# Stick-breaking attention: one scan over both sigmoids against differences of v, and the causal mask as a GpSimd product instead of a matmul

## The chip, the cores and the metric

The kernel runs on one core of a Trainium2 chip. The metric is the device time of one execution in microseconds (us), the median of the runs shown. Engines are named as in the profile: PE is TensorE (PEld its weight loads), DVE is VectorE, ACT is ScalarE, POOL is GpSimd, SP is SyncE, which here issues the DMAs.

## The reference

One layer of a streaming encoder: half a SwiGLU feed-forward, a mixer of two head groups, another half SwiGLU, and a closing norm, for 1024 prompt rows and 32 rows of a running stream. The change touches one head group, the stick-breaking attention: 8 heads of width 64, strictly causal, and for the running stream 128 cached keys ahead of its own 32.

```python
def sb_weights_apply(q, k, v, q_pos, k_pos):
    z = jnp.einsum('bqhd,bkhd->bhqk', q, k) * SB_SCALE
    causal = k_pos[None, :] < q_pos[:, None]
    log_fail = jnp.where(causal, jax.nn.log_sigmoid(-z), 0.0)
    after = lax.cumsum(log_fail, axis=3, reverse=True) - log_fail
    w = jnp.where(causal, jnp.exp(jax.nn.log_sigmoid(z) + after), 0.0)
    return jnp.einsum('bhqk,bkhd->bqhd', w, v)
```

So the weight of key k is sigmoid(z_k) times the product of sigmoid(-z_j) over the later visible keys j, and the output is the sum of the weights times the rows of v. v itself and the normed k are outputs too.

## The kernel before

Rows lie along the free axis: x is eight tiles of 128 features by 1056 rows (1024 of the prompt, 32 of the running stream). Matmuls with weights run in three products of split halves (`mm3`, lines 118 to 120) over three chunks of 352 rows.

The eight attention heads go in four pairs, p = 0 to 3. `sb_project` projects q, k and v of a pair, `sb_operands` splits q and k into high and low halves and loads the cache, and `sb_items` lists the work of a pair: for each of its two heads eight blocks of 128 queries, block i against the L = 128 (i + 1) keys up to its own. A block passes through three steps:

- `Block.scores` (lines 1588 to 1609): z = qk in one or two PSUM pieces of at most 512 columns (L1600, L1601); a third matmul per block adds a bfloat16 mask of -1e30 to the last 128 columns (L1603). ACT makes two sigmoids of each piece, f of -z (L1604) and w of z (L1605). DVE multiplies f up from the right in place (the scan, L1607), and then multiplies w by the product that starts one key later (L1608); a 1 behind the last column (the memset on POOL, L1595) is the empty product.
- `Block.turn`: PE transposes w, up to four 128-column pieces into one PSUM tile `tr` (L1619); ACT and DVE split it into a high and a low half `wt` (L109 and L113). There are two `tr` buffers, which the transposes of norms (L1124) and of v (L1142, L1149) share.
- `Block.values`: PE sums `wt` times the rows `vs` of v over two query blocks (L1632).

`Sample` does the same for the running stream with 160 keys (L1650 to L1664, mask matmul L1658). The scores of a block are listed three blocks ahead of its transposes. `run` mixes the list with filler for PE: the projections of the next pair, the gates of the other head group, and for the last pair the output projection (`out_group`). On that, a scheduler with its own cost model and the buffers of each pool sets the final order of every engine, so that an edit moves instructions that it doesn't name. Every engine then works its list strictly in that order.

Two things lie on POOL in this stage besides the memsets: the power -1/2 of the norms (L1046, nr from nv), for which it waits for DVE, and the copies that spread such a result over a tile (L1100).

v is projected in `put_v`: ACT copies the three chunks into `vf` (L1480), one DMA writes it out (L1482), and `rows_of` transposes it into `vs`. The cached v comes by one DMA per pair (L1567).

Of the kernel before, what the change touches and what calls it, by code (L numbers as in the profile page):

```python
# [7 lines left out]

F32 = mybir.dt.float32
F32R = mybir.dt.float32r  # L10
BF16 = mybir.dt.bfloat16
AF = mybir.ActivationFunctionType
ALU = mybir.AluOpType
PSUM = bass.MemoryType.PSUM

P = 128
# [13 lines left out]
def cs(c):  # L30
    return slice(c * CW, (c + 1) * CW)
# [1431 lines left out]
def sb_project(S, A, p, norms=()):  # L1463


    nc = S.nc
    T = Ctx()
    q = T.q = S.x[p]
    T.k = T.v = None

    def put_k(c, ps):
        if c == 0:
            T.k = S.stage.tile([P, NR], F32, name="kf", tag="kf")
            T.nk = Norm(S, T.k, S.ones64, 2, S.vec[:, 1:2])
        nc.scalar.activation(T.k[:, cs(c)], ps, AF.Copy)

    def put_v(c, ps):
        if c == 0:
            T.v = S.stage.tile([P, NR], F32, name="vf", tag="vf")
        nc.scalar.activation(T.v[:, cs(c)], ps, AF.Copy)  # L1480
        if c == NCH - 1:
            nc.sync.dma_start(A["v"][p], T.v)  # L1482

    def put_q(c, ps):
        if c == 0:
            T.sq = square_buf(S)
        nc.scalar.activation(T.sq[:, cs(c)], ps, AF.Square)
        nc.vector.tensor_scalar(q[:, cs(c)], ps, S.vec[:, 0:1], 0.125, op0=ALU.mult, op1=ALU.mult)

    def scales(r):  # L1490

        T.rq = r
# [89 lines left out]
class Block:  # L1582
# [5 lines left out]
    def scores(self):  # L1588
        S, T, h, i = self.S, self.T, self.h, self.i
        nc = S.nc  # L1590
        L = (i + 1) * P
        qs = slice(i * P, L)
        f = S.big.tile([P, NR], F32, name="f", tag="f")
        w = S.big.tile([P, SEQ], F32, name="w", tag="b")
        nc.gpsimd.memset(f[:, L : L + 1], 1.0)  # L1595
        n = L if L <= 512 else L // 2
        for s0 in range(0, L, n):
            z = S.pz.tile([P, 512], F32, name="z", tag="z")
            last = s0 + n == L
            nc.tensor.matmul(z[:, :n], T.qh[h][:, qs], T.ks[h][:, s0 : s0 + n], start=True, stop=False)  # L1600
            nc.tensor.matmul(z[:, :n], T.ql[h][:, qs], T.ks[h][:, s0 : s0 + n], start=False, stop=not last)  # L1601
            if last:
                nc.tensor.matmul(z[:, n - P : n], S.identb, S.maskb, start=False, stop=True)  # L1603
            nc.scalar.activation(f[:, s0 : s0 + n], z[:, :n], AF.Sigmoid, scale=T.rn[:, i, h : h + 1])  # L1604
            nc.scalar.activation(w[:, s0 : s0 + n], z[:, :n], AF.Sigmoid, scale=T.rq[:, i, h : h + 1])  # L1605
        fr = f[:, 0:L][:, ::-1]
        nc.vector.tensor_tensor_scan(fr, fr, fr, 1.0, op0=ALU.mult, op1=ALU.bypass)  # L1607
        nc.vector.tensor_mul(w[:, :L], w[:, :L], f[:, 1 : L + 1])  # L1608
# [27 lines left out]
class Sample:  # L1636
# [7 lines left out]
    def scores(self):  # L1644
        S, T, W = self.S, self.T, self.W
        nc = S.nc
        z = S.pz.tile([P, 512], F32, name="zs", tag="z")
        f = S.tmp.tile([DEC, 2, W + 1], F32, name="fs", tag="fs", bufs=1)
        w = self.w = S.tmp.tile([DEC, 2, W], F32, name="ws", tag="ws", bufs=1)
        nc.gpsimd.memset(f[:, :, W : W + 1], 1.0)  # L1650
        zv = z[:DEC, : 2 * W].rearrange("p (h s) -> p h s", h=2)
        for h in range(2):
            qh, ql, kn = T.qh[h][:, SEQ:NR], T.ql[h][:, SEQ:NR], T.ks[h][:, SEQ:NR]
            nc.tensor.matmul(zv[:, h, :PAST], qh, T.kc[:, h], start=True, stop=False)
            nc.tensor.matmul(zv[:, h, :PAST], ql, T.kc[:, h], start=False, stop=True)
# [80 lines left out]
def body(tc, A):  # L1736
# [10 lines left out]
    with ExitStack() as top:  # L1747
# [70 lines left out]
        with ExitStack() as es:  # L1818
# [37 lines left out]
            def chores(slots):  # L1856
                slots.later(20, lambda: nc.vector.tensor_copy(S.identb, consts[:, 0]))
                slots.later(20, lambda: nc.vector.tensor_copy(S.maskb, consts[:, 2]))
                splits.plan(slots)

            gate_up(S, H, op, steps, None, None, lambda p, xd: downs[0].head(p, xd), A["x"], chores, (R, done))
# [234 lines left out]
def constants():  # L2096
    i = np.arange(P)
    ident = np.eye(P, dtype=np.float32)
    ones64 = np.where(i[:, None] // 64 == i[None, :] // 64, 1.0 / 64, 0.0)
    causal = np.where(i[None, :] >= i[:, None], -1e30, 0.0)  # L2100
    consts = np.stack([ident, ones64, causal], 1).astype(np.float32)
    reset = np.ones((P, NR), np.float32)
    reset[:, ::P] = 0.0
    s, t = i[:, None], i[None, :]
    masks = [(s >> (lv + 1) == t >> (lv + 1)) & ((s >> lv) % 2 == 0) & ((t >> lv) % 2 == 1) for lv in range(5)]
    even = masks[1] & (s % 2 == 0)
    masks = np.stack([masks[0], even, masks[1] & ~even] + masks[2:] + [s == t], 1).astype(np.uint32)
    return consts, reset, masks


def layouts(i):
# [36 lines left out]
    a["cv"] = c(i["cache_sb_v"].reshape(PAST, 4, P).transpose(1, 0, 2))  # L2148
# [42 lines left out]
```

## Time and profile before

| | us |
|---|---|
| median of three runs | 2094.55 (2091.72 to 2094.66) |
| span of the profiled execution, first to last instruction | 2092.9 |
| the stage with the four head pairs, from about 960 to 1320 in the profile | 360 |
| PE busy in this stage | 344.85 |
| DVE, ACT and POOL busy in this stage | 267.27, 204.98, 55.17 |

The profiled execution is given by its span; its own device time isn't listed beside it, and the median lies 1.65 us above that span. In the profile a group of instructions has its line, engine, operation, out<-in by the program's names, shape and count, then busy us and mean ns of one, then the idle time of the engine just before them and what ended it. A row of the timeline has start, duration, engine, line and the idle time before it. PE's matmuls overlap, so the busy time of a matmul is longer than what it keeps the next one waiting; the step from start to start shows that.

### The profile page before, as it was taken

The page shows a single profiled execution, that of the slowest core. Times are in us where ns is not written, and L with a number is a line of the kernel's source. Part 1 is how long each engine was busy: PE and PEld are TensorE (multiplying, and loading weights), DVE is VectorE, ACT ScalarE, POOL GpSimd, SP SyncE. Part 2 cuts the span into 40 slices and gives each one's busy share as a digit, 9 for nine tenths or more (in the row PEclk, how much of TensorE's full clock was granted, in tenths as well). Part 3 has the DMA queues.
Part 4 walks back from the last instruction along what each step waited for, and adds up shares of the span by engine and source line. Part 5 has one row for each costly group of instructions (what it writes and reads, how often), then busy time and mean ns, then how long its engine had stood idle before and what let it go on. Part 6 is the DMA issues. An engine that isn't in the chain of part 4 may idle for free.

```text
span 2092.9 us, 39194 instructions
## 1 busy us (share of the span) xinstructions
PE 2044.0 (98%) x15746; PEld 1982.8 (95%) x15746; DVE 1432.4 (68%) x2232; ACT 881.1 (42%) x1628; POOL 663.2 (32%) x586
## 2 busy tenths in 40 slices
PE   7999999999999999999999999999999999999998
PEld 6999999999999988888999988999999999999998
DVE  6877777765776756377667588696776666566655
ACT  5444444442233442336555466454443433322233
POOL 0144434336773200121122101001343343367720
PEclk9999999999999999999999999999999999999999
DMA  6367667769853111213314162332673434398622
GB/s 233 101 233 260 245 249 258 258 234 399 326 198 117 53 61 61 75 35 88 113 51 119 51 186 90 101 103 76 226 257 142 155 134 153 130 399 315 230 111 74
DMA packets 140580, 350.65 MB, mean 168 GB/s; under 512 B 12904, under 2 KB 34824, under 8 KB 136816
## 3 DMA queue, kind: packets, MB, share of 16 engines
q1 hardware_dynamic: 139824, 347.61, 46.7%
q8 instruction: 124, 2.03, 0.4%
q10 hardware_dynamic: 576, 0.54, 0.1%
q14 instruction: 56, 0.46, 0.1%
HBM read 216.70 MB, written 124.65 MB: 163 GB/s over the span
## 4 chain that ended last, share of the span: by engine, by line
PE 88%; DVE 7%; ACT 2%; DMA 2%; issue 1%; SPq 0%; DVEq 0%; ACTq 0%
PE acc_c L473 11%; PE acc_d L473 11%; PE acc_a L473 11%; PE acc_b L473 5%; PE pd_d L822 4%; PE pd_a L822 4%; PE pd_c L822 4%; PE pj L118 4%; PE acc L381 4%; PE pj L120 4%; PE pj L119 4%; PE pd L118 2%; PE pd L119 2%; PE pd L120 2%; PE pd_b L822 2%; DVE f L1607 2%
## 5 line engine op out<-in xcount | busy, mean ns | idle before, releaser
L473 PE MATMUL acc_a<-h,whl 128*128 128x264 f32 x1920 | 247.4, 285 | 0.3 <-DVE whl L51 0.3
L473 PE MATMUL acc_d<-part,S 128*128 128x264 f32 x1920 | 247.6, 285 | 0.0
L473 PEld LDWEIGHTS acc_a<-h,whl 128*128 128x128 f32 x1920 | 239.6, 188 | 0.5 <-DVE whl L51 0.5
L473 PEld LDWEIGHTS acc_d<-part,S 128*128 128x128 f32 x1920 | 239.8, 188 | 0.1
L118 PE MATMUL pj<-h,whl 128*128 128x352 f32 x576 | 205.4, 357 | 0.0
L120 PE MATMUL pj<-h,whl 128*128 128x352 f32 x576 | 189.9, 330 | 0.0
L119 PE MATMUL pj<-h,whl 128*128 128x352 f32 x576 | 189.4, 329 | 0.0
L51 DVE TENSOR_TENSOR x<-x 128x528 fp32r<-128x528 f32 (+1 forms) x188 | 156.0, 845 | 19.1 <-ACT x L50 19.0
L50 ACT ACTIVATE x<-x 128x528 fp32r<-128x528 f32 (+1 forms) x188 | 117.3, 634 | 119.2 <-DVE x L546 37.2
L526 POOL TENSOR_TENSOR x<-tc,x 128x528 f32<-128x528 f32 x60 | 100.3, 1672 | 186.2 <-DVE tc L525 148.8
L473 PE MATMUL acc_c<-h,A 128*128 128x264 f32 x960 | 123.7, 285 | 0.6 <-DVE u L492 0.6
L444 POOL TENSOR_TENSOR s<-wraw 128x512 f32<-128x512 f32 x38 | 60.8, 1599 | 200.3 <-DVE S L113 134.9
L473 PE MATMUL acc_c<-part,S 128*128 128x264 f32 x960 | 124.1, 285 | 0.0
L473 PE MATMUL acc_b<-h,S 128*128 128x264 f32 x960 | 123.6, 285 | 0.0
L473 PEld LDWEIGHTS acc_c<-h,A 128*128 128x128 f32 x960 | 119.7, 188 | 0.8 <-issue 0.8
L473 PEld LDWEIGHTS acc_c<-part,S 128*128 128x128 f32 x960 | 120.0, 188 | 0.0
L473 PEld LDWEIGHTS acc_b<-h,S 128*128 128x128 f32 x960 | 119.8, 188 | 0.0
L118 PEld LDWEIGHTS pj<-h,whl 128*128 128x128 f32 x576 | 110.1, 191 | 6.3 <-issue 2.5
L51 DVE TENSOR_TENSOR S<-s,S 128x512 fp32r<-128x512 f32 x152 | 114.1, 751 | 0.6 <-ACT S L50 0.6
L840 POOL TENSOR_TENSOR x<-x,u 128x528 f32<-128x528 f32 x64 | 98.3, 1553 | 45.3 <-DVE x L811 45.3
L119 PEld LDWEIGHTS pj<-h,whl 128*128 128x128 f32 x576 | 110.5, 192 | 1.0 <-issue 0.3
L50 ACT ACTIVATE S<-s 128x512 fp32r<-128x512 f32 x152 | 93.6, 623 | 42.0 <-POOL s L447 17.9
(389 smaller groups left out, 4869.8 us busy)
## 6 DMA issues: line engine op xcount, KB each, us to landing
part_spill<-x SPq DMA_DIRECT2D x112, 528.0 KB, 3.7
h<-part_spill SPq DMA_DIRECT2D x64, 528.0 KB, 10.7
part<-part_spill SPq DMA_DIRECT2D x48, 528.0 KB, 10.7
win_split<-x SPq DMA_DIRECT2D x44, 512.0 KB, 3.6
whl<-win_split SPq DMA_DIRECT2D x22, 1024.0 KB, 4.9
wraw<-w1g SPq DMA_DIRECT2D x22, 512.0 KB, 5.1
wraw<-w1u SPq DMA_DIRECT2D x22, 512.0 KB, 6.2
x<-win SPq DMA_DIRECT2D x44, 256.0 KB, 2.9
```

The source lines that it names most:

```text
L50: self.later(k, lambda: nc.scalar.activation(hi, src, AF.Copy))
L51: self.later(k + 1, lambda: nc.vector.tensor_sub(lo, src, hi.bitcast(F32)))
L118: nc.tensor.matmul(out, w[:, 0, wsl], a[:, 0, asl], start=first, stop=False)
L119: nc.tensor.matmul(out, w[:, 0, wsl], a[:, 1, asl], start=False, stop=False)
L120: nc.tensor.matmul(out, w[:, 1, wsl], a[:, 0, asl], start=False, stop=last)
L381: nc.tensor.matmul(out, self.w[i](k, a), quarter(S, k, b, j), start=k == 0 and n == 0, stop=k == KT - 1 and n == 2)
L444: eng.tensor_add(self.s1, a21, a22)
L473: nc.tensor.matmul(t[:, s, :SW], w[:, a, ks], m(k, b, s), start=fresh and k == 0 and n == 0, stop=k == 3 and n == 2, skip_group_check=not ...
L526: nc.gpsimd.tensor_mul(two(hid), t, sg)
L822: nc.tensor.matmul(t[:, s, :SW], w[:, u, k * P : k * P + P], b[:, v, ss(s)], start=fresh and k == 0 and i == 0, stop=k == 1 and i == 2, sk ...
L840: nc.gpsimd.tensor_add(x[r][h], x[r][h], u)
L1607: nc.vector.tensor_tensor_scan(fr, fr, fr, 1.0, op0=ALU.mult, op1=ALU.bypass)
```

## The change

With f = 1 - s (s the other sigmoid), the recurrence G_k = f_k G_(k+1) + s_k from the right gives the sum of all weights from key k on. The weight is G_k - G_(k+1), so the output is the sum of G_k times (v_k - v_(k-1)). The scan therefore takes both sigmoids (multiply by f, add w) and writes G into w; the transposes and the matmuls with v use G, and the rows of v are replaced by differences of neighbouring rows.

- In each block POOL multiplies the last 128 columns of w by a 0/1 mask (L1614 of the new file), the mask matmul goes, and so do the multiplication L1608 and the memset L1595. f needs no mask, since a masked w leaves the state of the scan at 0. The sample does likewise, with two products of 32 columns and no L1664.
- v goes through a new tile `vt`, one column wider than the chunk, that carries the last column of the chunk before. POOL copies that column, and takes the differences into `vf` (one 352-wide or 320-wide subtraction per chunk, and two short ones where the running stream begins, which use the last cached row, `cvl`). `v_out` is now written in three DMAs per pair out of `vt`.
- The cached v comes twice, once shifted by a row, in two DMAs, and POOL subtracts the one from the other.
- f has two buffers instead of three. The bfloat16 copies of the identity and the mask go (two DVE casts early in the program).

```diff
     def put_v(c, ps):
...
-        nc.scalar.activation(T.v[:, cs(c)], ps, AF.Copy)
-        if c == NCH - 1:
-            nc.sync.dma_start(A["v"][p], T.v)
+        t = S.tmp.tile([P, 1 + CW], F32, name="vt", tag="vt")
+        if c == 0:
+            nc.gpsimd.memset(t[:, 0:1], 0.0)
+        else:
+            nc.gpsimd.tensor_copy(t[:, 0:1], T.part[:, CW:])
+        nc.scalar.activation(t[:, 1:], ps, AF.Copy)
+        nc.sync.dma_start(A["v"][p][:, cs(c)], t[:, 1:])
+        n = CW if c < NCH - 1 else SEQ - c * CW
+        nc.gpsimd.tensor_sub(T.v[:, c * CW : c * CW + n], t[:, 1 : n + 1], t[:, :n])
+        if n < CW:
+            nc.gpsimd.tensor_sub(T.v[:, SEQ : SEQ + 1], t[:, n + 1 : n + 2], S.cvl[:, p : p + 1])
+            nc.gpsimd.tensor_sub(T.v[:, SEQ + 1 :], t[:, n + 2 :], t[:, n + 1 : CW])
+        T.part = t
...
-    cv = S.tmp.tile([P, P], F32, name="cv", tag="cv", bufs=1)
-    nc.sync.dma_start(cv, A["cv"][p])
-    put(T.vc, cv.unsqueeze(1))
+    cv = S.tmp.tile([P, 2, P], F32, name="cv", tag="cv", bufs=1)
+    for i in range(2):
+        nc.sync.dma_start(cv[:, i], A["cv"][p][i : i + PAST])
+    nc.gpsimd.tensor_sub(cv[:, 1], cv[:, 1], cv[:, 0])
+    put(T.vc, cv[:, 1:])
...
-        f = S.big.tile([P, NR], F32, name="f", tag="f")
+        f = S.big.tile([P, NR], F32, name="f", tag="f", bufs=2)
         w = S.big.tile([P, SEQ], F32, name="w", tag="b")
-        nc.gpsimd.memset(f[:, L : L + 1], 1.0)
...
-            nc.tensor.matmul(z[:, :n], T.ql[h][:, qs], T.ks[h][:, s0 : s0 + n], start=False, stop=not last)
-            if last:
-                nc.tensor.matmul(z[:, n - P : n], S.identb, S.maskb, start=False, stop=True)
+            nc.tensor.matmul(z[:, :n], T.ql[h][:, qs], T.ks[h][:, s0 : s0 + n], start=False, stop=True)
             nc.scalar.activation(f[:, s0 : s0 + n], z[:, :n], AF.Sigmoid, scale=T.rn[:, i, h : h + 1])
             nc.scalar.activation(w[:, s0 : s0 + n], z[:, :n], AF.Sigmoid, scale=T.rq[:, i, h : h + 1])
-        fr = f[:, 0:L][:, ::-1]
-        nc.vector.tensor_tensor_scan(fr, fr, fr, 1.0, op0=ALU.mult, op1=ALU.bypass)
-        nc.vector.tensor_mul(w[:, :L], w[:, :L], f[:, 1 : L + 1])
+        nc.gpsimd.tensor_mul(w[:, qs], w[:, qs], S.mask)
+        wr = w[:, :L][:, ::-1]
+        nc.vector.tensor_tensor_scan(wr, f[:, :L][:, ::-1], wr, 0.0, op0=ALU.mult, op1=ALU.add)
```

The scheduler's order changes from the first block of pair 0 to the end of the attention; ahead of that and behind it PE's order is the same. Lines of the changed file are up to 12 away from those before: L112 there is L113 here, L1045 is L1046, L1099 is L1100.

The list of DVE at the third to fifth block of pair 1 (keys 384, 512, 640) before; `f` and `w` are the sigmoids, `wt` the split of the transposed weights:

```order
L1607 SCALAR_TENSOR_TENSOR f<-f 128x384
L1608 TENSOR_TENSOR w<-w,f 128x384
L113 TENSOR_TENSOR wt<-tr,wt 128x128
L1607 SCALAR_TENSOR_TENSOR f<-f 128x512
L1608 TENSOR_TENSOR w<-w,f 128x512
L113 TENSOR_TENSOR wt<-tr,wt 128x2x128
L1607 SCALAR_TENSOR_TENSOR f<-f 128x640
L113 TENSOR_TENSOR wt<-tr,wt 128x3x128
```

And in the changed kernel, at the same place:

```order
L1616 SCALAR_TENSOR_TENSOR w<-f,w 128x384
L112 TENSOR_TENSOR wt<-tr,wt 128x128
L1616 SCALAR_TENSOR_TENSOR w<-f,w 128x512
L112 TENSOR_TENSOR wt<-tr,wt 128x2x128
L1616 SCALAR_TENSOR_TENSOR w<-f,w 128x640
L112 TENSOR_TENSOR wt<-tr,wt 128x3x128
```

The multiplication is gone, and each split of an earlier block (128 columns belong to the first block, 2x128 to the second) stands directly behind a scan.

POOL's list around the same place before, from the end of pair 0: seven memsets are those of the last two blocks of pair 0 and the first five of pair 1, and L1046 with its two copies is a norm of the filler:

```order
L1042 MEMSET nv 128x18
L1595 MEMSET f 128x1 x7
L1046 TENSOR_TENSOR nr<-nv,mhalf 128x18
L1100 COPY x<-nr 128x1024
L1100 COPY nL<-nr 32x128
L1042 MEMSET nv 128x9
```

In the changed kernel; L1614 is the mask product, and the first three of them belong to the last block of pair 0 and the first two of pair 1:

```order
L1488 TENSOR_TENSOR vf<-vt 128x320
L1490 TENSOR_TENSOR vf<-vt,cvl 128x1
L1491 TENSOR_TENSOR vf<-vt 128x31
L1614 TENSOR_TENSOR w<-w,consts 128x128 x3
L1045 TENSOR_TENSOR nr<-nv,mhalf 128x18
L1099 COPY x<-nr 128x1024
L1099 COPY nL<-nr 32x128
L1614 TENSOR_TENSOR w<-w,consts 128x128
L1041 MEMSET nv 128x9
L1614 TENSOR_TENSOR w<-w,consts 128x128 x3
```

The mask product of the third block of pair 1 (384 keys) stands behind the norm's power and both copies, where before only memsets stood.

More of the change, by code (lines that the diff above doesn't have):

```diff
@@ L10 @@
 F32R = mybir.dt.float32r
-BF16 = mybir.dt.bfloat16
 AF = mybir.ActivationFunctionType
@@ L1130, in square_buf @@
 def square_buf(S):
-    return S.nbuf[0] if S.nbuf else S.big.tile([P, NR], F32, name="sqb", tag="f")
+    return S.nbuf[0] if S.nbuf else S.big.tile([P, NR], F32, name="sqb", tag="f", bufs=2)
 def rows_of(S, src, put):
@@ L1598, in scores @@
             z = S.pz.tile([P, 512], F32, name="z", tag="z")
-            last = s0 + n == L
             nc.tensor.matmul(z[:, :n], T.qh[h][:, qs], T.ks[h][:, s0 : s0 + n], start=True, stop=False)
-            nc.tensor.matmul(z[:, :n], T.ql[h][:, qs], T.ks[h][:, s0 : s0 + n], start=False, stop=not last)
-            if last:
-                nc.tensor.matmul(z[:, n - P : n], S.identb, S.maskb, start=False, stop=True)
+            nc.tensor.matmul(z[:, :n], T.ql[h][:, qs], T.ks[h][:, s0 : s0 + n], start=False, stop=True)
             nc.scalar.activation(f[:, s0 : s0 + n], z[:, :n], AF.Sigmoid, scale=T.rn[:, i, h : h + 1])
             nc.scalar.activation(w[:, s0 : s0 + n], z[:, :n], AF.Sigmoid, scale=T.rq[:, i, h : h + 1])
-        fr = f[:, 0:L][:, ::-1]
-        nc.vector.tensor_tensor_scan(fr, fr, fr, 1.0, op0=ALU.mult, op1=ALU.bypass)
-        nc.vector.tensor_mul(w[:, :L], w[:, :L], f[:, 1 : L + 1])
+        nc.gpsimd.tensor_mul(w[:, qs], w[:, qs], S.mask)
+        wr = w[:, :L][:, ::-1]
+        nc.vector.tensor_tensor_scan(wr, f[:, :L][:, ::-1], wr, 0.0, op0=ALU.mult, op1=ALU.add)
         self.w = w
@@ L1647, in scores @@
         z = S.pz.tile([P, 512], F32, name="zs", tag="z")
-        f = S.tmp.tile([DEC, 2, W + 1], F32, name="fs", tag="fs", bufs=1)
+        f = S.tmp.tile([DEC, 2, W], F32, name="fs", tag="fs", bufs=1)
         w = self.w = S.tmp.tile([DEC, 2, W], F32, name="ws", tag="ws", bufs=1)
-        nc.gpsimd.memset(f[:, :, W : W + 1], 1.0)
         zv = z[:DEC, : 2 * W].rearrange("p (h s) -> p h s", h=2)
@@ L1656, in scores @@
             nc.tensor.matmul(zv[:, h, PAST:], qh, kn, start=True, stop=False)
-            nc.tensor.matmul(zv[:, h, PAST:], ql, kn, start=False, stop=False)
-            nc.tensor.matmul(zv[:, h, PAST:], S.identb[:DEC, :DEC], S.maskb[:DEC, :DEC], start=False, stop=True)
+            nc.tensor.matmul(zv[:, h, PAST:], ql, kn, start=False, stop=True)
         for h in range(2):
-            nc.scalar.activation(f[:, h, :W], zv[:, h], AF.Sigmoid, scale=T.rn[:DEC, NB, h : h + 1])
+            nc.scalar.activation(f[:, h], zv[:, h], AF.Sigmoid, scale=T.rn[:DEC, NB, h : h + 1])
             nc.scalar.activation(w[:, h], zv[:, h], AF.Sigmoid, scale=T.rq[:DEC, NB, h : h + 1])
-            fr = f[:, h, 0:W][:, ::-1]
-            nc.vector.tensor_tensor_scan(fr, fr, fr, 1.0, op0=ALU.mult, op1=ALU.bypass)
-        nc.vector.tensor_mul(w, w, f[:, :, 1 : W + 1])
+            nc.gpsimd.tensor_mul(w[:, h, PAST:], w[:, h, PAST:], S.mask[:DEC, :DEC])
+            wr = w[:, h][:, ::-1]
+            nc.vector.tensor_tensor_scan(wr, f[:, h][:, ::-1], wr, 0.0, op0=ALU.mult, op1=ALU.add)
     def turn(self):
@@ L1757, in body @@
         consts = const.tile([P, 3, P], F32, name="consts")
-        S.ident, S.ones64 = consts[:, 0], consts[:, 1]
-        S.identb = const.tile([P, P], BF16, name="identb")
-        S.maskb = const.tile([P, P], BF16, name="maskb")
+        S.ident, S.ones64, S.mask = (consts[:, n] for n in range(3))
         S.ones128 = const.tile([P, P], F32, name="ones128")
@@ L1763, in body @@
         S.vec = const.tile([P, 4], F32, name="vec")
+        S.cvl = const.tile([P, 4], F32, name="cvl")
         S.mhalf = const.tile([P, 2 * NB + 2], F32, name="mhalf")
@@ L1843, in body @@
             nc.sync.dma_start(S.vec, A["vec"])
+            nc.sync.dma_start(S.cvl, A["cvl"])
             downs = []
@@ L1854, in body @@
             splits = Splits(S, halves_of(jobs), (S.x[2], S.x[3]))
[L1856 to L1861, printed above, removed]
+            gate_up(S, H, op, steps, None, None, lambda p, xd: downs[0].head(p, xd), A["x"], splits.plan, (R, done))
             down = downs[0]
@@ L2099, in constants @@
     ones64 = np.where(i[:, None] // 64 == i[None, :] // 64, 1.0 / 64, 0.0)
-    causal = np.where(i[None, :] >= i[:, None], -1e30, 0.0)
+    causal = np.where(i[None, :] < i[:, None], 1.0, 0.0)
     consts = np.stack([ident, ones64, causal], 1).astype(np.float32)
@@ L2147, in layouts @@
     a["ck"] = c(i["cache_sb_k"].reshape(PAST, 4, P).transpose(1, 2, 0))
-    a["cv"] = c(i["cache_sb_v"].reshape(PAST, 4, P).transpose(1, 0, 2))
+    a["cv"] = c(np.pad(i["cache_sb_v"].reshape(PAST, 4, P).transpose(1, 0, 2), ((0, 0), (1, 0), (0, 0))))
+    a["cvl"] = c(i["cache_sb_v"].reshape(PAST, 4, P)[-1].T)
     a["state"] = i["state_gla"].reshape(2, P, P)
```

## The prediction, made before the changed kernel was run

> **What bounds the kernel now.** I read the page first, then the busy times of the stage with the attention, then the groups of instructions and the waits of that stage, and last the timeline at single places.
>
> ```profile
> span 2092.9 us, 39194 instructions
> PE 2044.0 (98%) x15746; PEld 1982.8 (95%) x15746; DVE 1432.4 (68%) x2232; ACT 881.1 (42%) x1628; POOL 663.2 (32%) x586
> ```
>
> PE is busy for 98% of the span. The change acts between about 960 and 1320 us, where the four head pairs lie; columns are the stretch, its length, and busy us of PE, PEld, DVE, ACT and POOL.
>
> ```profile
> 960.00:1320.00 360.00, 344.85 (x2343) 319.44 (x2342) 267.27 (x432) 204.98 (x445) 55.17 (x99) 0.99 0.31 94
> ```
>
> Here too PE is nearly full: 360 - 344.85 = 15.15 us are idle. So there are two ways to gain: issue less on PE, or take from the 15.15. Who makes PE wait:
>
> ```profile
> PE tr L1619 <- DVE wt L113: 5.4, 8, 1.6
> PE tr L1124 <- DVE wt L113: 4.1, 4, 1.7
> ...
> DVE f L1607 <- ACT f L1604: 22.3, 26, 2.0
> ```
>
> Nearly all of PE's own waits are for a `tr` buffer that DVE has not yet split into `wt`. DVE is late because scans and products stand in its list ahead of the split. DVE itself waited 22.3 us, 26 times, for ACT's first sigmoid: in these cases the scan stood at the head of its list and was not ready.
>
> **What goes from PE.** 64 mask matmuls in the blocks, 8 in the sample. A matmul's busy time overlaps its neighbours, so I take steps from start to start:
>
> ```profile
> 1024.77 0.40 PE L1601 MATMUL z<-ks,ql 128*128 128x512 f32 x1
> 1025.01 0.39 PE L1600 MATMUL z<-ks,qh 128*128 128x512 f32 x1
> ...
> 1025.23 0.40 PE L1601 MATMUL z<-ks,ql 128*128 128x512 f32 x1
> 1025.47 0.23 PE L1603 MATMUL z<-maskb,identb 128*128 128x128 bf16 x1
> 1025.51 0.41 PE L118 MATMUL pj<-h,whl 128*128 128x352 f32 x1
> 1025.75 0.32 PE L119 MATMUL pj<-h,whl 128*128 128x352 f32 x1
> ...
> 1026.07 0.32 PE L118 MATMUL pj<-h,whl 128*128 128x352 f32 x1
> 1026.23 0.32 PE L119 MATMUL pj<-h,whl 128*128 128x352 f32 x1
> ```
>
> Without a mask in between, L1601 keeps its follower 1025.01 - 1024.77 = 0.24 us, and L118 keeps L119 0.16 us: 0.40 together. With it, from L1601 to L119, it is 1025.75 - 1025.23 = 0.52. The mask matmul costs 0.12 us, though it is only 0.04 us until the next start: the rest is a slower first step behind it. 72 of them at 0.12 make 8.6 us. Bounds: 72 x 0.04 = 2.9 us below; above, the mean of a whole one (0.23, next row) x 64 = 14.7 us.
>
> ```profile
> L1603 PE MATMUL z<-maskb,identb 128*128 128x128 bf16 x64 | 14.7, 230 | 0.0
> L1607 DVE TENSOR_TENSOR_SCAN f<-f 128x128 f32<-128x128 f32 (+3 forms) x64 | 87.5, 1367 | 22.8 <-ACT f L1604 22.3
> L1608 DVE TENSOR_TENSOR w<-w,f 128x128 f32<-128x128 f32 (+3 forms) x64 | 49.4, 771 | 3.8 <-ACT f L1604 0.2
> L1605 ACT ACTIVATE w<-z,nr 128x384 f32<-128x384 f32 (+4 forms) x96 | 56.0, 584 | 0.0
> L1229 DVE TENSOR_TENSOR_SCAN B<-reset,B 128x1056 f32<-128x1056 f32 x2 | 4.7, 2358 | 0.1
> ...
> 1027.17 2.29 DVE L1607 TENSOR_TENSOR_SCAN f<-f 128x1024 f32<-128x1024 f32 x1 [0.24 <-ACT f L1604]
> 1029.49 0.69 DVE L113 TENSOR_TENSOR wt<-tr,wt 128x512 fp32r<-128x512 f32 x1
> ```
>
> **What goes from DVE, and what the scan then waits for.** The 64 products L1608 go, 49.4 us of DVE. The new scan has the form of L1229 (two inputs, multiply and add): 2358 ns for 1056 columns is 2.23 ns each, and 2.29 us for 1024 is the same, so the 87.5 us stay. But the scan must now wait for the second sigmoid as well (0.58 us, so far hidden beside the scan) and for the mask product on POOL. POOL's nearest rows:
>
> ```profile
> L786 POOL TENSOR_TENSOR s<-wraw 128x256 f32<-128x256 f32 x32 | 24.4, 764 | 22.4 <-DMA wraw<-w1d 12.5 <-DMA wraw<-w2d 10.0
> L111 POOL TENSOR_TENSOR h<-hf,h 128x352 fp32r<-128x352 f32 x12 | 13.4, 1124 | 66.6 <-ACT h L109 66.6
> L1046 POOL TENSOR_TENSOR nr<-nv,mhalf 128x18 f32<-128x18 f32 x11 | 37.8, 3433 | 54.2 <-DVE nv L1044 54.2
> ```
>
> 128 columns are half of L786's 256: an estimate between 0.38 (half of 764) and 0.76 us; I take 0.5. A free scan thus starts 0.58 + 0.5 = 1.1 us later than now and the block is done 1.1 - 0.77 = 0.3 us later on the mean, while DVE at the head of its list stands idle for what it used to compute. For the transposes that is harmless where they lie some us behind. It hurts where a split stands directly behind a long scan, as at 1029.49 above, where PE was already waiting. There are eight scans of 1024 columns; I put 2 us on PE for them (nothing if PE's slack holds, 8 x 1.1 = 9 us if all hit).
>
> Against that, DVE has 49.4 us less to do. It gains where DVE runs without a gap, as in the last block of all, where the next split comes behind the product:
>
> ```profile
> 1308.41 0.67 DVE L113 TENSOR_TENSOR wt<-tr,wt 128x512 fp32r<-128x512 f32 x1
> 1308.99 1.22 DVE L1608 TENSOR_TENSOR w<-w,f 128x1024 f32<-128x1024 f32 x1
> ```
>
> I take 5 of the 15.15 us back, what four such products last (4 x 1.22); bounds 0 and, with all of PE's waiting gone, 15.
>
> f has two buffers instead of three, so ACT's first sigmoid of a block waits for the scan two blocks earlier. Where blocks follow every 2 to 3 us that can hold ACT, and the copies listed behind; I put 1 us, between 0 and 3.
>
> **POOL's list.** So far it hardly mattered when POOL did anything in a block. Now 64 scans wait for it, and in its list some of the masks stand behind a norm's power and its two copies. The third block of pair 1 before:
>
> ```profile
> 1051.30 3.22 POOL L1046 TENSOR_TENSOR nr<-nv,mhalf 128x18 f32<-128x18 f32 x1 [2.10 <-DVE nv L1044]
> 1054.58 1.46 POOL L1100 COPY x<-nr 128x1024 f32<-128x1024 f32 x1
> 1055.98 0.75 POOL L1100 COPY nL<-nr 32x128 f32<-32x128 f32 x1
> ...
> 1052.09 0.57 ACT L1605 ACTIVATE w<-z,nr 128x384 f32<-128x384 f32 x1
> ...
> 1052.22 0.96 DVE L1607 TENSOR_TENSOR_SCAN f<-f 128x384 f32<-128x384 f32 x1 [0.38 <-ACT f L1604]
> 1053.31 0.56 DVE L1608 TENSOR_TENSOR w<-w,f 128x384 f32<-128x384 f32 x1
> ...
> 1051.10 0.34 PE L1601 MATMUL z<-ks,ql 128*128 128x384 f32 x1
> ...
> 1055.56 0.49 PE L1619 MATMUL tr<-consts,w 128*128 128x128 f32 x3
> ```
>
> w is ready at 1052.66, but the mask comes only behind the last copy, at about 1056.7, and ends at 1057.2; the scan of 384 columns takes 0.96 us, so the transposes that ran at 1055.56 can run at about 1058.2: PE waits 2.6 us. The split of the first block stands behind that scan too. Pair 2 has the same order; there I put 1.5 us, a choice between nothing and the same. The others of the eleven powers stand where a later block's mask is not yet due or its transposes lie several blocks off; 1 us together. POOL: 5 us, between 0 (masks slip in ahead, or PE's slack covers it) and 11 x 2.6 = 29 us.
>
> **The differences of v.** POOL gets 12 subtractions of about 1.1 us (L111's row) and small ones. ACT writes the last chunk, and the transposes of v follow:
>
> ```profile
> 951.87 0.46 ACT L1480 ACTIVATE vf<-pj 128x352 f32<-128x352 f32 x1
> 955.14 0.60 PE L1142 MATMUL tr<-consts,vf 128*128 128x128 f32 x4
> ...
> 1024.26 0.46 ACT L1480 ACTIVATE vf<-pj 128x352 f32<-128x352 f32 x1 [0.15 <-PE pj L120]
> 1043.77 0.60 PE L1142 MATMUL tr<-consts,vf 128*128 128x128 f32 x4
> ```
>
> From the ACT's end it is 2.8 us in pair 0 and 19 us in pair 1, so 1.1 to 1.5 us of POOL are covered; I cost them at nothing. Without that cover it would be 4 x 1.5 = 6 us. The three `v_out` DMAs and the second cache DMA are on SP, whose later entries are weights loaded far ahead; nothing. What does count is that a subtraction, or the wait for a chunk, can stand in POOL's list ahead of a mask; that is within the 5 us.
>
> Sum: -8.6 (PE) - 5 (DVE) + 2 (splits behind scans) + 1 (f) + 5 (POOL) = -5.6 us. The span goes from 2092.9 to 2087.3; the median lies 1.65 us above the span, so 2089.0 us in round numbers.
>
> **A rule that speaks against it.** Two products of one size next to each other:
>
> ```profile
> 970.57 0.69 DVE L1608 TENSOR_TENSOR w<-w,f 128x512 f32<-128x512 f32 x1
> ...
> 1055.34 1.25 DVE L1608 TENSOR_TENSOR w<-w,f 128x512 f32<-128x512 f32 x1
> ```
>
> The second ran while POOL copied (1055.98 above) and took 0.56 us longer. The Trainium skill, page "SBUF — State Buffer", section "Who interferes with whom", says that a VectorE instruction with two SBUF inputs and a GpSimd instruction that reads SBUF lock each other out for a whole instruction, the later one waiting. By that rule, to which these two rows agree, the memsets before were harmless and the new masks and subtractions are not.
>
> **Rivals.**
>
> *Scans and POOL take turns* (that rule at work). A mask that comes during another block's scan ends only behind it, and a subtraction holds a scan. Then each of the 64 masks adds its 0.5 us to DVE's chain: 32 of the 49.4 us are given back, DVE's relief of 5 us becomes about 2, and with the 12 subtractions delaying some scans PE gets 1 us more to wait. -5.6 + 4 = -1.6: 2093.0 us. For it: the row of 1.25. Against it: a scan that is next in line can't start before the one ahead ends anyway.
>
> *DVE was the brake.* Splits come sooner, PE's waits mostly go, and POOL's powers fall into slack: -8.6 - 8 = -16.6, about 2078.0 us. For it: PE's waits are for DVE. Against it: the scan now starts 1.1 us later and waits for two engines.
>
> *POOL becomes the brake, slower.* If every power in front of a mask stops DVE for its 3.4 us and more, and PE for 2 us on the mean over eleven of them, that is 22 us instead of 5: -5.6 + 17 = +11.4, about 2106.0 us. It decides from (8.6 + 5 - 3 + 4.2) / 11 = 1.3 us of PE per power. For it: from z (1051.10) to the transposes (1055.56) PE leaves the third block 4.5 us, and power and copies alone take 5.4. Against it: scores are listed three blocks ahead, and with 22.3 us of waiting already at the head of DVE's list PE itself waited 1.7 us at most.
>
> **How the numbers follow.** A measurement of this kernel tells 0.2% from no change, 4.2 us: faster is below 2090.4, slower above 2098.7. Chances: the forecast 0.45, of which two thirds end below 2090.4; DVE as the brake 0.15; taking turns 0.20, of which a tenth ends below 2090.4; POOL as the brake 0.20, of which a tenth stays within 0.2%. Faster: 0.30 + 0.15 + 0.02 = 0.47; slower: 0.18; same: 0.35. The bounds of the terms, which don't all meet, and most of the rivals give 2079 to 2100; beyond lie the ends of the first and last case, about 0.2 together.
>
> **What would show it.** Right: no L1603; PE's z steps shorter by 0.12 a block; scans at 2.23 ns a column; DVE busy in the stage lower by about 50 us, with more waiting for POOL's w; PE idle in the stage between 15 and 22 us, the new waits at the third blocks of pairs 1 and 2. Wrong: scans that take longer than 2.29 us for 1024 columns, PE's idle time below 10 or above 25 us, waits of PE for vf, or a time above 2098.7 us.

## The result, and the profile after

| | before | after |
|---|---|---|
| median, us | 2093.6 (2091.72 to 2094.66, 4 runs) | 2110.0 (2109.39 to 2111.77, 4 runs) |
| ratio to before | | 1.008 (95%: 1.0069 to 1.0092) |
| span of the profiled execution, us | 2092.9 | 2107.6 |

The change makes the kernel slower by 16.4 us. The prediction said 2089.0 us, with bounds of 2079 and 2100. All times here are medians of fast runs; one run further below, of before without the mask, was slow (2196.46 us at a clock of 0.849) and is not counted. The last PE instruction of the attention ends at 1317.96 us before and at 1333.40 after, 15.4 us later; in all the spans of the two profiled executions differ by 14.7. So the loss arises in the attention. The same stretch as in the prediction, after the change, in the same columns (stretch, length, busy us of PE, PEld, DVE, ACT, POOL, granted clock):

```profile
960.00:1320.00 360.00, 330.13 (x2174) 312.57 (x2173) 214.26 (x351) 198.11 (x433) 95.71 (x132) 0.96 0.30 91
```

PE is idle for 360 - 330.13 = 29.9 us where it was 15.15; the limit that the prediction set for "wrong" was 25. DVE is busy for 53 us less, as foreseen. POOL has 40 us more, and the granted clock is 0.96 in place of 0.99. Who waits for whom between 960 and 1340 us, with the total in us, the number of waits and the longest; PE's rows are put first:

```profile
PE tr L1627 <- DVE wt L112: 10.1, 7, 2.3
PE av L1640 <- DVE wt L112: 4.5, 3, 3.2
PE tr L1123 <- DVE wt L112: 4.4, 3, 1.9
PE tr L1677 <- DVE wt L112: 4.2, 1, 4.2
...
DVE w L1616 <- POOL w L1614: 67.8, 42, 4.8
DVE w L1616 <- POOL nv L1041: 4.4, 1, 4.4
POOL nr L1045 <- DVE nv L1043: 36.0, 10, 9.3
```

Read upwards from the scan's rows. The scan (L1616) waits 72 us for POOL, where the scan before waited 22.3 us for ACT. DVE works its list in order, so the split of other blocks' transposes (L112) stands behind the waiting scan, and PE waits for the split. Two groups of the same stretch tell why POOL is late:

```profile
L1616 DVE TENSOR_TENSOR_SCAN w<-f,w 128x128 f32<-128x128 f32 (+3 forms) x64 | 88.9, 1391 | 72.5 <-POOL w L1614 67.8 <-POOL nv L1041 4.4
L1614 POOL TENSOR_TENSOR w<-w,consts 128x128 f32<-128x128 f32 x64 | 31.4, 492 | 210.9 <-ACT w L1613 210.8
L1045 POOL TENSOR_TENSOR nr<-nv,mhalf 128x18 f32<-128x18 f32 (+1 forms) x11 | 35.5, 3227 | 36.1 <-DVE nv L1043 36.0
```

The mask itself takes 0.49 us, as estimated, and the scan is as long as it was (1391 ns on the mean, 1367 before). But eleven powers of 3.2 us on the mean (nine of 18 columns at 3.5 us, two of 9 columns at 1.8) stand in the same list as the masks. One of the places, the twelfth block of pair 1, where the transposes fell back by 5.5 us against before:

```profile
1105.31 3.22 POOL L1045 TENSOR_TENSOR nr<-nv,mhalf 128x18 f32<-128x18 f32 x1 [2.00 <-DVE nv L1043]
...
1106.24 0.68 ACT L1613 ACTIVATE w<-z,nr 128x512 f32<-128x512 f32 x1
...
1108.59 1.04 POOL L1099 COPY x<-nr 128x1024 f32<-128x1024 f32 x1
1108.68 0.28 PE L1640 MATMUL av<-wt,vs 128*128 128x256 f32 x1
...
1109.57 0.28 POOL L1099 COPY nL<-nr 32x128 f32<-32x128 f32 x1
...
1109.87 0.86 POOL L1614 TENSOR_TENSOR w<-w,consts 128x128 f32<-128x128 f32 x2
1110.35 1.46 DVE L1616 TENSOR_TENSOR_SCAN w<-f,w 128x512 f32<-128x512 f32 x1 [4.79 <-POOL w L1614]
1111.73 0.39 DVE L112 TENSOR_TENSOR wt<-tr,wt 128x256 fp32r<-128x256 f32 x1
...
1112.18 0.90 PE L1640 MATMUL av<-wt,vs 128*128 128x256 f32 x3 [3.22 <-DVE wt L112]
```

w is ready at 1106.92, the mask begins at 1109.87, behind the power and its two copies. DVE stands for 4.79 us at the scan, a split that PE needs stands behind it, and PE issues nothing from 1108.7 to 1112.2. Then a second price follows. Four single microseconds and the seven behind them, in the columns of the stretch above:

```profile
1109.00:1110.00 1.00, 0.00 (x0) 0.00 (x0) 0.00 (x0) 0.31 (x1) 1.00 (x4) 1.00 0.00 0
1110.00:1111.00 1.00, 0.00 (x0) 0.00 (x0) 0.65 (x1) 0.00 (x0) 0.73 (x2) 1.00 0.00 0
1111.00:1112.00 1.00, 0.00 (x0) 0.00 (x0) 1.00 (x2) 0.00 (x0) 0.00 (x0) 0.64 0.04 8
1112.00:1113.00 1.00, 0.82 (x4) 0.82 (x5) 1.00 (x2) 0.00 (x0) 0.00 (x0) 0.50 0.00 0
...
1112.00:1119.00 7.00, 6.82 (x28) 6.73 (x29) 3.20 (x5) 3.36 (x7) 0.46 (x1) 0.56 0.01 2
```

The third column from the right is PE's clock. The trace has it at half from 1111.3 to 1118.1 us, so PE comes back to half speed. It looks busy there, but does less: three of the 128x256 matmuls of `av` take 0.90 us at 1112.18, where thirteen took 1.65 at 1102.77, at full clock.

### The profile page after: what moved, and what is told of

Read it like the earlier page. It is cut to its first block, busy times and chain, and to the rows that moved or that the text cites. A ratio compares the mean times of both kernels' runs of the same rounds, so it can differ in the third digit from the quotient of the medians.

```text
span 2107.6 us, 38968 instructions
## 1 busy us (share of the span) xinstructions
PE 2041.6 (97%) x15674; PEld 1987.2 (94%) x15674; DVE 1385.6 (66%) x2162; ACT 881.3 (42%) x1628; POOL 708.7 (34%) x626
## 4 chain that ended last, share of the span: by engine, by line
PE 87%; DVE 5%; ACT 2%; issue 2%; DMA 2%; POOL 2%; SPq 0%; DVEq 0%; POOLq 0%; ACTq 0%
PE acc_a L472 11%; PE acc_c L472 11%; PE acc_d L472 11%; PE acc_b L472 5%; PE pd_d L821 4%; PE pd_a L821 4%; PE pd_c L821 4%; PE pj L117 4%; PE acc L380 4%; PE pj L118 4%; PE pj L119 4%; PE pd L117 2%; PE pd L119 2%; PE pd L118 2%; PE pd_b L821 2%
## 5 line engine op out<-in xcount | busy, mean ns | idle before, releaser
L50 DVE TENSOR_TENSOR x<-x 128x528 fp32r<-128x528 f32 (+1 forms) x188 | 156.1, 846 | 19.3 <-ACT x L49 19.2
L1616 DVE TENSOR_TENSOR_SCAN w<-f,w 128x128 f32<-128x128 f32 (+3 forms) x64 | 88.9, 1391 | 72.5 <-POOL w L1614 67.8
```

The source lines that it names most:

```text
L50: self.later(k + 1, lambda: nc.vector.tensor_sub(lo, src, hi.bitcast(F32)))
L1616: nc.vector.tensor_tensor_scan(wr, f[:, :L][:, ::-1], wr, 0.0, op0=ALU.mult, op1=ALU.add)
```

## The experiments

Theory 1: the mask product in POOL's list, behind long instructions, holds the scan; the scan at the head of DVE's list holds the splits; PE waits. Rivals: A, f has only two buffers; B, the v differences and their waits hold POOL; C, the scan has to wait for the second sigmoid in any case. Ratios are to before, on the same chip. The last two columns split the mean span into what the granted clock can have taken at most, span x (1 - mean clock), and the rest. The clock is on record to three digits, so the split of one run is good to 1 us. Edits are shown in part; the lines left out are named or marked by three dots.

| kernel | median us | ratio (95%) | clock's part, us | rest, us |
|---|---|---|---|---|
| before (four sets of 11 to 29 runs) | 2092.6 to 2094.6 | 1 | 9.1 to 10.2 | 2082.2 to 2082.7 |
| after | 2110.0 | 1.0080 (1.0069 to 1.0092) | 20.0 | 2088.5 |
| after, mask by matmul | 2090.6 | 0.9982 (0.9974 to 0.9991) | 10.3 | 2078.3 |
| after, mask on DVE | 2090.7 | 0.9983 (0.9975 to 0.9992) | 13.4 | 2075.7 |
| after, power left out | 2086.9 | 0.9965 (0.9952 to 0.9978) | 10.0 | 2075.4 |
| before, power left out | 2092.3 | 0.9989 (0.9981 to 0.9998) | 9.3 | 2081.2 |
| after, power in three | 2101.1 | 1.0032 (1.0019 to 1.0044) | 15.1 | 2083.4 |
| before, with POOL product | 2109.6 | 1.0080 (1.0064 to 1.0096) | 14.8 | 2093.9 |
| after, v differences on DVE | 2112.6 | 1.0090 (1.0077 to 1.0104) | 20.6 | 2090.3 |
| before, no mask | 2090.4 | 0.9985 (0.9976 to 0.9994) | 10.1 | 2078.3 |
| after, root on DVE | 2100.4 | 1.0028 (1.0019 to 1.0038) | 15.9 | 2082.9 |
| the same, w first | 2092.8 | 0.9990 (0.9981 to 1.0000) | 13.2 | 2077.5 |
| before, two f buffers | 2095.2 | 1.0001 (0.9991 to 1.0012) | 10.8 | 2082.2 |
| after, mask on DVE, w first | 2086.7 | 0.9959 (0.9946 to 0.9972) | 10.4 | 2074.3 |

**The mask back on PE.**

```diff
...
+                nc.tensor.matmul(z[:, n - P : n], S.identb, S.maskb, start=False, stop=True)
...
-        nc.gpsimd.tensor_mul(w[:, qs], w[:, qs], S.mask)
```

The sample and the constants go back likewise.

> After, but with the causal mask put back as a matmul of -1e30 on PE; POOL has no mask product, the scan, the two f buffers and the v differences stay. Theory 1 (the mask product in POOL's list holds the scan, the scan holds the splits, PE waits): the 67.8 us that scans wait for POOL go to zero, PE's idle time between 960 and 1320 us falls from 29.9 to under 20 us, the low-clock stretches become as few as before (6.8 us lost or less), and the time is 2084 to 2094 us although the matmuls cost some 8.6 us. Rival A (the two f buffers): ACT and the scans still wait, over 2100 us. Rival B (the v differences and their waits on POOL): the v transposes and PE still wait, over 2100 us. Rival C (a scan that must wait for the second sigmoid at all, at the head of DVE's list): scans wait for ACT w for over 50 us and the time stays above 2100 us.

Measured: 2090.6 us, 19 us less than after. No scan waits for POOL; PE's idle time is 12.2 us:

```profile
960.00:1320.00 360.00, 347.78 (x2382) 323.77 (x2381) 221.23 (x368) 206.81 (x448) 60.97 (x61) 0.99 0.30 93
```

The scans now wait for the second sigmoid:

```profile
DVE w L1619 <- ACT w L1617: 45.4, 44, 2.3
```

Two f buffers, the v differences and the wait for w are all still there, and the kernel is faster than before. So neither A nor B nor C makes the loss by itself.

**The mask on DVE.**

```diff
-        nc.gpsimd.tensor_mul(w[:, qs], w[:, qs], S.mask)
+        nc.vector.tensor_mul(w[:, qs], w[:, qs], S.mask)
```

The sample likewise.

> After, but with the mask product on DVE, in front of the scan, instead of on POOL. Theory 1: no scan waits for POOL, DVE gets 64 products of 128x128 (0.2 to 0.3 us each, 13 to 19 us of the 53 that it was relieved of), no mask matmul on PE; PE's idle time between 960 and 1320 us falls to 10 to 18 us and the time to 2076 to 2090 us. Rivals A to C (f's buffers, v differences, the wait for the second sigmoid): the product now waits for the second sigmoid at the head of DVE's list, nothing else is cured, and the time stays above 2100 us.

Measured: 2090.7 us, just above theory 1's range, with PE idle for 17.7 us. On DVE the product is shorter than on POOL, and the 19.2 us of the 64 take part of DVE's relief:

```profile
L1614 DVE TENSOR_TENSOR w<-w,consts 128x128 f32<-128x128 f32 x64 | 19.2, 300 | 35.2 <-ACT w L1613 34.8
```

**The power left out, in after and in before.** Order and number of all instructions stay.

```diff
-    nc.gpsimd.tensor_tensor(r.rearrange("p b g -> p (b g)"), v, S.mhalf[:, :n], op=ALU.pow)
+    nc.gpsimd.tensor_tensor(r.rearrange("p b g -> p (b g)"), v, S.mhalf[:, :n], op=ALU.mult)
```

> After, with the power of the norms on POOL replaced by a plain product of the same operands: the power is left out of the computation, the order on all engines is the same. If the 3.2 us of the powers are what holds the masks behind them, each of the eleven gives back some 3 us to the mask behind it and the loss of 16 us shrinks to under 6: 2094 to 2100 us, with most of the low-clock stretches gone. If what holds POOL is its own waiting in order (for DVE's nv, 36.0 us in 10 waits, and for ACT's vt, 16.9 us), the waits stay and the time falls by less than 5 us: 2105 to 2110.

> Control: before, with the same power left out. No block waits for POOL there, only a norm's apply and the sigmoid scales do: 2090 to 2094 us, within 0.2% of before. If it gains more than 4 us, the powers were in the path before the change too, and the gain of the same edit in after counts only by the difference.

Measured: after falls to 2086.9 us, 23 us less and lower than either theory gave; before only by 0.11%, 2.3 us. The place shown above, in this kernel:

```profile
1102.24 0.23 POOL L1045 TENSOR_TENSOR nr<-nv,mhalf 128x18 f32<-128x18 f32 x1 [2.00 <-DVE nv L1043]
1102.53 1.04 POOL L1099 COPY x<-nr 128x1024 f32<-128x1024 f32 x1
...
1103.17 0.68 ACT L1613 ACTIVATE w<-z,nr 128x512 f32<-128x512 f32 x1
...
1103.93 0.46 POOL L1614 TENSOR_TENSOR w<-w,consts 128x128 f32<-128x128 f32 x1
1104.43 1.23 DVE L1616 TENSOR_TENSOR_SCAN w<-f,w 128x512 f32<-128x512 f32 x1 [1.94 <-POOL w L1614]
```

POOL still waits for DVE's nv (42.1 us in the stretch) and the scans still wait 48.0 us for POOL, in waits of at most 2.6 us. So what cost was the power, and not the sum of the waits. Whether it was the length of one instruction or POOL's load, which falls with it by 31 us, this run can't tell; the power in three, below, can.

**One part alone, in before.** POOL multiplies and the mask matmul stays; besides, one early operation on DVE makes the 0/1 mask.

```diff
+        nc.gpsimd.tensor_mul(w[:, qs], w[:, qs], S.mask)
         fr = f[:, 0:L][:, ::-1]
```

> One part alone: before, with a product on POOL (w of the diagonal block times a mask of 0 and 1, which changes no value, since the mask matmul has made those elements 0) between the second sigmoid and the product on DVE. Scan, three f buffers, mask matmul and v are as before. Theory 1: this alone brings the loss, and as nothing is relieved, more of it: PE idle over 28 us between 960 and 1320 us, 2106 to 2125 us. Rivals A and B (f buffers, v differences): 2092 to 2098 us.

Measured: 2109.6 us; this product alone, with the order that the scheduler makes for it, brings the whole loss to a kernel with three f buffers and no v differences. PE's idle time between 960 and 1320 us is 24.5 us, not over 28; in the table the rest grew by 11.7 us and the clock's part by 5.7. The places are not all those of after: the third, fourth and twelfth blocks of pair 1 fall back by 5 us together, where after's did by 8.9. How much of this loss is the powers' wasn't measured. Here POOL's product takes 858 ns, where after's took 492:

```profile
L1606 POOL TENSOR_TENSOR w<-w,consts 128x128 f32<-128x128 f32 x64 | 54.9, 858 | 145.1 <-ACT w L1605 144.6 <-issue 0.2
```

**The v differences on DVE.**

```diff
-        nc.gpsimd.tensor_sub(T.v[:, c * CW : c * CW + n], t[:, 1 : n + 1], t[:, :n])
+        nc.vector.tensor_sub(T.v[:, c * CW : c * CW + n], t[:, 1 : n + 1], t[:, :n])
...
-    nc.gpsimd.tensor_sub(cv[:, 1], cv[:, 1], cv[:, 0])
+    nc.vector.tensor_sub(cv[:, 1], cv[:, 1], cv[:, 0])
```

> After, with the subtractions for the v differences (and for the cached v) on DVE instead of POOL; POOL keeps the one-column copies, the powers and the masks. Theory 1: the powers are still in front of the masks; the subtractions took 12 us of POOL and made it wait for ACT 16.9 us, so some masks come sooner: 2103 to 2111 us. Rival B (the v differences are what holds POOL): below 2098 us.

Measured: 2112.6 us, just above theory 1's range, and no gain (its interval overlaps after's). Rival B falls a second time.

**Before without the mask.**

```diff
-            if last:
-                nc.tensor.matmul(z[:, n - P : n], S.identb, S.maskb, start=False, stop=True)
...
```

The sample likewise.

> Before, without the 72 mask matmuls: the causal mask is left out. This prices the first term of the sum by itself: 72 x 0.12 = 8.6 us less, 2083 to 2087 us, if PE is the bound there; if PE's time is given back at its waits for splits, 2088 to 2093 us.

Measured: 0.15% less, 3.1 us (1.3 to 5.0), not 8.6. From 960 us to the end of the attention, before first:

```profile
960.00:1317.96 357.96, 342.81 (x2331) 317.56 (x2331) 266.35 (x430) 203.53 (x443) 55.17 (x99) 0.99 0.31 95
```

and without the mask:

```profile
960.00:1313.29 353.29, 334.18 (x2259) 314.35 (x2258) 265.87 (x429) 202.29 (x443) 54.69 (x99) 0.99 0.31 96
```

PE is busy for 8.6 us less, but idle for 19.1 us in place of 15.15: 4.0 us come back as waiting. The attention ends 4.7 us earlier in this one execution.

**Two buffers for f, in before.**

```diff
-        f = S.big.tile([P, NR], F32, name="f", tag="f")
+        f = S.big.tile([P, NR], F32, name="f", tag="f", bufs=2)
```

The squares of the norms (`square_buf`) share these buffers and get two as well, as in after.

> One part alone: before, with two buffers for f instead of three. Rival A in the old kernel: ACT's first sigmoid waits for the product two blocks earlier. By theory 1 it costs 0 to 3 us (the prediction put 1 us): 2092 to 2097 us. If f's buffers had a large part in the loss, over 2100 us.

Measured: 1.0001 (0.9991 to 1.0012): no difference.

**The power in three.** Each third behind the matmuls that make its columns.

```diff
+    nc.gpsimd.tensor_tensor(hold["r"].rearrange("p b g -> p (b g)")[:, c], v[:, c], S.mhalf[:, c], op=ALU.pow)
...
+            if root is None:
+                rsqrt_part(S, hold, groups, b0)
             if b0 == 6:
-                put((root or rsqrt)(S, hold["st"], groups))
+                put(root(S, hold["st"], groups) if root else hold["r"])
```

> After, with each norm's power on POOL cut in three, each third right behind the three matmuls that make its columns, so that masks can go in between; the computation is whole. The parts should take 3.2 / 3 = 1.1 us each. Theory 1 with the powers' length as what holds the masks (after it fell from 2110 to 2086.9 us when the power was a product): 2086 to 2096 us, POOL's longest hold in front of a mask below 2.5 us, low-clock stretches as before. If it is POOL's total load or its waits in order and not the length of one instruction, three waits for nv in place of one make it no better: 2104 to 2114 us.

Measured: 2101.1 us, between the two. A third takes 1.43 us, not 1.1:

```profile
L1063 POOL TENSOR_TENSOR nr<-nv,mhalf 128x6 f32<-128x6 f32 x27 | 38.6, 1432 | 86.4 <-DVE nv L1059 78.9 <-DVE nv L1061 6.1 <-PE z L1630 1.5
```

Of after's excess of 6 us in the table's last column 5 are gone, of its excess in the clock's only half: in this kernel's trace the clock is at half from 983.7 to 997.3 us, behind a PE wait of 2.1 us in pair 0. POOL is busy for 103.7 us in the stage, 8 more than in after, and still 9 us of the loss are gone: so it was the length of one instruction more than POOL's load.

**The root on DVE, then w ahead of f.** The first takes the power from POOL for good; the second is the first with this:

```diff
+            nc.scalar.activation(w[:, s0 : s0 + n], z[:, :n], AF.Sigmoid, scale=T.rq[:, i, h : h + 1])
+            if s0 + n == L:
+                nc.gpsimd.tensor_mul(w[:, qs], w[:, qs], S.mask)
             nc.scalar.activation(f[:, s0 : s0 + n], z[:, :n], AF.Sigmoid, scale=T.rn[:, i, h : h + 1])
-            nc.scalar.activation(w[:, s0 : s0 + n], z[:, :n], AF.Sigmoid, scale=T.rq[:, i, h : h + 1])
-        nc.gpsimd.tensor_mul(w[:, qs], w[:, qs], S.mask)
```

> After, with the norms' power moved from POOL to DVE: one operation on the bits for a first guess of the reciprocal root and three Newton steps, ten operations of 128x18 at an estimated 0.1 to 0.15 us each, 1.0 to 1.5 us in place of 3.5 us on POOL; the computation is whole. Theory 1: the masks come as soon as with the power left out (2086.9 us), DVE gets 11 x 1.3 = 14 us back of the 53 it was relieved of: 2085 to 2093 us, faster than before or equal to it. If DVE's extra chain delays the splits as POOL did, 2095 to 2106 us.

> As the kernel with the root on DVE, and in each block the last part's second sigmoid w comes ahead of its first sigmoid f, so that the mask product on POOL (0.49 us) runs beside the sigmoid of f. The scan's wait for POOL's w was 48.0 us with the power left out, in 45 waits; up to 0.5 us of each goes: 15 to 22 us less waiting at the head of DVE's list. If these short waits cost PE anything, 2082 to 2088 us; if only the long holds behind powers did, the same as with the root on DVE alone, within 3 us.

Measured: 2100.4 and 2092.8 us, the first in the range for a DVE chain that delays the splits, the second above its 2082 to 2088. The ten operations take 0.18 us each, 1.8 us per root, longer than estimated:

```profile
L1051 DVE SCALAR_TENSOR_TENSOR nt<-nt,nv 128x18 f32<-128x18 f32 (+1 forms) x33 | 6.2, 189 | 1.0
L1050 DVE TENSOR_TENSOR nt<-nr 128x18 f32<-128x18 f32 (+1 forms) x33 | 5.9, 178 | 0.8
L1052 DVE SCALAR_TENSOR_TENSOR nr<-nt,nr 128x18 f32<-128x18 f32 (+1 forms) x33 | 5.8, 175 | 1.0
```

In the trace of the first, the first block's transposes come 9.5 us later than before and the last av only 7.0, so the attention itself got 2.5 us shorter; about 5 of the 9.5 are a stretch at half clock from 956 to 966 us. Why it falls there is open. With w ahead of f 7.6 us go, more than the 3 that would have meant nothing: the short waits at the head of DVE's list cost some us too.

**A version that beats both**: mask on DVE, w's sigmoid ahead of f's.

> A version meant to beat both: the mask product on DVE (the kernel with it there took 2090.7 us) and, in each block's last part, w's sigmoid ahead of f's, so that DVE multiplies while ACT still computes f. DVE waited 34.8 us in 37 waits for w at that product. If those short waits at the head of DVE's list cost PE something, 2083 to 2089 us; if DVE then only waits for f in the same place, 2089 to 2093 us.

Measured: 2086.7 us, 0.41% (0.28 to 0.54) below before, within the range for short waits that cost something. One wait of PE for 2.3 us, at the ninth block of pair 2, is still in it and is explained below. DVE multiplies while ACT computes f:

```profile
L1614 DVE TENSOR_TENSOR w<-w,consts 128x128 f32<-128x128 f32 x64 | 19.4, 302 | 23.6 <-ACT w L1612 23.0
```

## Why the prediction was wrong

*POOL, +5 us: this step failed.* At the third block of pair 1 it was right: the prediction had the mask end at 1057.2 and the transposes run at 1058.2 with 2.6 us of waiting on PE. After has this:

```profile
1056.85 0.45 POOL L1614 TENSOR_TENSOR w<-w,consts 128x128 f32<-128x128 f32 x1
...
1057.33 1.23 DVE L1616 TENSOR_TENSOR_SCAN w<-f,w 128x384 f32<-128x384 f32 x1 [4.40 <-POOL nv L1041]
...
1058.80 0.55 PE L1627 MATMUL tr<-consts,w 128*128 128x128 f32 x3 [2.35 <-DVE wt L112]
```

The transposes of the third block of pair 2, for which it put 1.5 us, fell back by 0.8. What failed is the sentence on the other powers: "a later block's mask is not yet due or its transposes lie several blocks off; 1 us together". It looked at the block whose mask waits. The price is paid by other blocks: the waiting scan is first in DVE's list, and the splits behind it are due at once. So, the half clock behind each wait included, the transposes of the twelfth block of pair 1 fell back by 5.5 us, those of the seventh of pair 2 by 3.9 and those of the sixth of pair 3 by 2.9. Measured by leaving the power out, the term is 1.0080 - 0.9965, 1.15% or 24 us, 22 beyond what the same edit brings in before. That is 2 us for each of the eleven on the mean, the price of the rival "POOL becomes the brake", whose time, 2106.0 us, is the nearest of the four. The rival had the path right; that its price came out is luck in part. Five of the eleven powers cost 4 to 5 us each against the kernel without powers (in one trace of each), the others 1.4 at most, and the half clock, which the rival didn't have, is in these figures. What spoke against the rival, PE waits of 1.7 us at most, came from a trace in which the scans waited for ACT, for 2.0 us at most.

One of the five is not a mask's. At the ninth block of pair 2 (`avs` is the running stream's sum with v) before and after have:

```profile
1191.54 3.25 POOL L1046 TENSOR_TENSOR nr<-nv,mhalf 128x18 f32<-128x18 f32 x1
...
1192.22 0.18 DVE L1579 TENSOR_TENSOR x<-avt,avs 64x32 f32<-64x32 f32 x1 [0.77 <-ACT avt L1578]
...
1194.86 0.07 DVE L1025 MEMSET nv<- 128x18 f32 x1 [2.46 <-POOL nr L1046]
```

```profile
1201.06 3.57 POOL L1045 TENSOR_TENSOR nr<-nv,mhalf 128x18 f32<-128x18 f32 x1 [0.58 <-DVE nv L1043]
...
1201.89 0.19 ACT L1590 ACTIVATE avt<-avs 64x32 f32<-64x32 f32 x1 [1.58 <-PE avs L1694]
...
1204.69 0.15 DVE L1591 TENSOR_TENSOR x<-avt,avs 64x32 f32<-64x32 f32 x1 [3.11 <-issue]
...
1204.90 0.61 PE L1692 MATMUL avs<-wc,vc 128*128 128x32 f32 x2 [2.26 <-DVE x L1591]
```

In after x is ready at 1202.08 but runs only when the power is over, and PE waits for it. Ahead of x DVE's list now has the memset of the next norm's `nv` (L1024; L1025 before), which waits for the power, as the row at 1194.86 shows; before, it stood behind x. (The order is seen with the power left out, where the memset starts at 1192.06 and x at 1192.50; in after their starts are 0.01 us apart.) So here the power holds DVE without a mask. The same hold, PE wait and half clock are in the kernels with the mask on PE and on DVE, in before with POOL's product and in the last version, and this block's transposes fall back by 3.2 to 4.1 us in all five; with the v differences on DVE, where x comes first, they gain 1.6. This is the scheduler's order, which no run set by itself.

*The clock: a term that was missing.* Of the 16.4 us about 10 are clock (20.0 against 9 to 10 us in the table) and 6 the rest. In the trace of after, the half-clock stretches between 955 and 1400 us last 30.7 us in sum, which at half clock is 15.4 us of PE's time; those of before last 13.7, which is 6.8. In after, seven steps from one start on PE to the next are 2.2 us or longer, and with six of them a stretch began during the step or within 5 us behind it; in all fourteen traces it was so with 23 of 33. So a long PE wait in this kernel often costs more than itself.

*PE, -8.6 us: a size that was off.* Without the mask matmuls PE is busy for 8.6 us less, but 4 of it come back as waiting, and 3.1 us is what the time shows.

*DVE -5, splits +2, f +1: right, within its uncertainty.* Together they are -2 us. Everything but the move of the mask was measured at -3.8 us (-5.4 to -1.9) with the mask on PE, and f's buffers alone at +0.2 (-1.9 to +2.5). DVE and splits were not priced apart. With -3.1 for the mask matmuls that makes -6.9; the kernel without powers has -7.3, of which 2.3 are what the same edit brings in before. With the powers' 24 the sum is +17.

*The v differences, nothing: right.* No wait of PE for vf, and no gain from moving them.

*Scans and POOL take turns: seen, but not the cause of the loss.* The scans got longer by 1.4 us in all, though single ones did by up to 0.5 us (one of 768 columns took 2.31 in place of 1.76). POOL's side shows it more: in before with POOL's product, 35 of the 64 products took more than 0.5 us, and 33 of these ended 0.25 us behind the end of a scan that was running when they began, which makes the mean of 858 ns. In after only 4 of 64 took longer than 0.5 us. The Trainium skill, page "SBUF — State Buffer", section "Who interferes with whom", lets the later instruction of the two engines wait. These products, which came later than the scan, agree with it.

Of the signs that the prediction named for being right, DVE's 53 us less, scans of 2.29 us at 1024 columns and the stall at the third block of pair 1 came true; of those for being wrong, PE's idle time above 25 us and the time above 2098.7.

## What to carry to other kernels

Before a short step that others wait for is put on a lightly used engine, look for the longest instruction in that engine's list, not at its load: here, masks of 0.49 us shared a list with eleven powers of 3.2 us, on an engine that was busy for a quarter of the stage, and leaving the powers out gave 23 us back. The price is paid by whatever stands behind the waiting instruction in the list of its engine, so ask which engine then runs dry, and ask what a wait of 2 us and more does to PE's clock. Look also at what the scheduler moves: a memset ahead of an instruction that it has nothing to do with went with 3 to 4 us of delay in five kernels. Time saved on the engine that seems full is worth less than its sum where that engine also waits: 8.6 us came out as 3.

## What the runs showed of the hardware

- The stretches at half clock around the attention last 3.4, 6.8, 10.2 or 13.7 us in all fourteen traces. Between 950 and 1400 us there are 41, and 24 of them begin during a step of 2.0 us or more from one PE start to the next, or within 5 us behind it; some steps of 2.0 to 2.8 us have none behind them, and before's stretch at 1192.8 us has no PE wait above 1 us in the 15 us ahead of it. The Trainium skill, page "TensorE: Matmul & The Clock Gate", section "HAM oscillation — how this bites in real kernels", has a rule against PE gaps above some 3.4 us; here stretches came behind shorter ones too, though its window of 3.4 us is the step of these lengths. What besides waits starts a stretch stays open.
- Part of the spread between runs of one kernel goes with the clock: the mask-by-matmul kernel ran from 2087.0 us at a mean clock of 0.997 to 2095.3 us at 0.993. Its span x clock varied by 4.9 us where the time varied by 8.3. In after and in before without the mask, though, span x clock varied by more than the time.
- POOL's power has a fixed part: 18 columns took 3.2 us in most places and up to 4.7, 9 columns 1.8, 6 columns 1.3 in most and 1.43 on the mean, 3 columns 0.85 in most. From the most frequent of these an estimate is 0.4 us and 0.16 us for each column.
